# One weight sum of a seven-product output projection stored whole, and split into its two parts later

## The chip, the cores and the metric

The kernel runs on one core of a Trainium2 chip. The time is the device time of one execution in microseconds (us); the kernel before took 1030.03 us, the median of three runs (1028.07 to 1033.39). The engines are TensorE (PE; its weight loads are listed as PEld), VectorE (DVE), ScalarE (ACT), GpSimd (POOL) and SyncE (SP), which here issues most of the DMAs.

## What is computed

One block of a hybrid model on a sequence of 1024 tokens of width 1024, in float32. A state-space branch (SSD) and an attention branch of eight heads each give 1024 columns; the two stand side by side and go through an output projection, whose result is added to the input and normalized:

```python
mixed = jnp.concatenate([y_ssd, y_attn.astype(h.dtype)], axis=-1)   # 1024 x 2048
h = h + jnp.einsum('bse,ed->bsd', mixed, w_out[layer])              # w_out: 2048 x 1024
return rms_norm(h, final_norm_gain)
```

The change is in that projection alone.

## The kernel before

**Precision in two parts.** A float32 matrix product is made of three matmuls. Each operand is split into a high part, rounded to the engine's fp32r format by an ACT copy, and a low part, the operand less its high part, by a DVE subtraction. The sum high x high + high x low + low x high is gathered in PSUM. `product` (L854) does this for a tile of 128 tokens by 512 columns: eight steps k of three matmuls (L863, L864, L865), 24 in all; a product of four tiles has 96.

**Seven products.** The projection is taken as a 2 x 2 block product with seven block products in place of eight. The right operands are three quarters of w_out as they are (b11, b21, b22) and four sums T1 to T4 of quarters: T3 = b22 - b12, T2 = T3 + b11, T4 = b21 - T2, T1 = b22 - T2. The left operands are quarters of the transposed `mixed` and sums S1 to S4 of them. At the end stand, in this order, the products a12 x b21, S3 x T3 (its last two tiles), S2 x T2, S1 x T1, S4 x b22 and a22 x T4.

**Where the sums are made.** `sums_t(k)` (L695) makes T1 to T4 for rows 128k to 128k+127 of the quarters. It is a generator; the loop over the heads calls `next_sums` (L739) between the query tiles of attention, so the sums are made piece by piece from about 370 to 790 us. T1, T2 and T4 are split there by `split` (L702): an ACT copy to the high part (L704), its store to DRAM (L705), a DVE subtraction to the low part (L706), its store (L707). T3 is stored whole (L711). Behind T come the sums of the left operand S3 (`sums_s`, L723), in the same four buffers of tag K.

**How they come back.** `load_b` (L779) loads stored parts straight into two tiles of 128 x 8 x 512 of tag u (four of those exist, so a right operand can be loaded when the one two products back is done): eight DMAs of 512 KB. `prep_b` (L766) loads a whole operand in pieces of two k (512 KB) into raw tiles, and splits each piece by an ACT copy (L774) and a DVE subtraction (L775). There are two raw tiles, so the third piece is loaded when the first is split. T3 and the plain quarters go through `prep_b`, T1, T2 and T4 through `load_b`.

**Order.** The program is written in one order, and a planner that simulates time (L1052) then sets the order in which each engine takes its instructions; on the chip each engine keeps to it. All loads of the end go through `dma_next` (L753), in a chain on SP in the order in which they are written. The last attention head's output is needed in S2 as well, so a part of S2 is made late (L672, `s2`). `add` (L937) adds a finished product to the output rows `xr` and frees its PSUM buffer, of which there are two (`mm`); `end_p2` (L966) does it for a12 x b21, the loop at L980 for S2 x T2.

Of the kernel before, what the change touches and what calls it, by code (L numbers as in the profile page):

```python
# [8 lines left out]
F32 = mybir.dt.float32  # L9
# [6 lines left out]
P = 128  # L16
# [4 lines left out]
HALF = 512  # L21
# [17 lines left out]
def kernel(  # L39
# [12 lines left out]
    dma = nc.sync.dma_start  # L52
# [5 lines left out]
    dram = ctx.enter_context(tc.tile_pool(name="dram", bufs=1, space=bass.MemoryType.DRAM))  # L58
# [13 lines left out]
    def tH(shape, dt=F32, name="tH"):  # L72
        return big_tile("H", 5, shape, dt, name)

    def tK(shape, dt=F32, name="tK"):
        return big_tile("K", 4, shape, dt, name)
# [605 lines left out]

    NB = 8

    t_d = {n: dram.tile([NB, P, HALF] if n == 3 else [NB, 2, P, HALF], F32, name=f"t_d{n}") for n in (1, 2, 3, 4)}
    s3_d = dram.tile([NB, P, HALF], F32, name="s3_d")

    def w_quarter(kh, nh):
        src = w_out2[kh * D : (kh + 1) * D, nh * HALF : (nh + 1) * HALF]
        return src.rearrange("(a p) c -> a p c", p=P)  # L690

    def pin(ins):
        return tc.keep_in_program_order(ins)

    def sums_t(k):  # L695

        b11, b12, b21, b22 = (tK([P, HALF], name=f"b{i}{j}{k}") for i in range(1, 3) for j in range(1, 3))
        for raw, i, j in ((b22, 1, 1), (b12, 0, 1), (b11, 0, 0), (b21, 1, 0)):
            pin(dma(raw, w_quarter(i, j)[k]))
        yield  # L700

        def split(n, b):  # L702
            hi = tH([P, HALF], F32R, f"t{n}h{k}")
            A.activation(hi, b, AF.Copy)  # L704
            dma(t_d[n][k, 1], hi.bitcast(F32))  # L705
            V.tensor_tensor(b.bitcast(F32R), b, hi.bitcast(F32), ALU.subtract)  # L706
            dma(t_d[n][k, 0], b)  # L707

        t1, t2, t3, t4 = b22, b11, b12, b21
        pin(V.tensor_tensor(t3, t1, t3, ALU.subtract))  # L710
        dma(t_d[3][k], t3)  # L711
        V.tensor_tensor(t2, t3, t2, ALU.add)
        yield
        pin(V.tensor_tensor(t4, t4, t2, ALU.subtract))
        V.tensor_tensor(t1, t1, t2, ALU.subtract)
        yield
        split(2, t2)
        yield
        split(4, t4)
        split(1, t1)  # L720
        yield

    def sums_s():  # L723
# [11 lines left out]
        yield  # L735

    sums = [sums_t(k) for k in range(NB)] + [sums_s()]

    def next_sums():  # L739
# [13 lines left out]
    def dma_next(dst, src):  # L753

        if queued and queued[0] is not None:
            with tc.issue_after(queued[0]):
                queued[0] = dma(dst, src).ins
        else:
            ins = dma(dst, src).ins
            if queued:  # L760
                queued[0] = ins

    def b_tiles(name):
        return [big_tile("u", 4, [P, NB, HALF], F32R, f"{name}_{n}") for n in ("hi", "lo")]

    def prep_b(name, src, makers):  # L766

        hi, lo = b_tiles(name)
        k = 0
        for make, n in makers:  # L770
            raw = make([P, n, HALF], name=f"r{name}{k}")
            dma_next(raw, src[k : k + n].rearrange("a p c -> p a c"))
            cut = slice(k, k + n)
            A.activation(hi[:, cut, :], raw, AF.Copy)  # L774
            V.tensor_tensor(lo[:, cut, :], raw, hi[:, cut, :].bitcast(F32), ALU.subtract)  # L775
            k += n
        return hi, lo

    def load_b(name, parts):  # L779

        hi, lo = b_tiles(name)
        for k in range(0, NB, 2):
            for n, part in ((1, hi), (0, lo)):
                dma_next(part[:, k : k + 2, :].bitcast(F32), parts[k : k + 2, n].rearrange("a p c -> p a c"))
        return hi, lo
# [11 lines left out]
    def prep_a(name, q, cuts, piece):  # L797

        hi = big_tile("whi", 2, [P, NB, 256], F32R, f"{name}h{q}")
        lo = big_tile("wlo", 2, [P, NB, 256], F32R, f"{name}l{q}")  # L800
        for k0, k1 in zip(cuts, cuts[1:]):
            raw = piece(q, k0, k1 - k0)
            cut = slice(k0, k1)
            A.activation(hi[:, cut, :], raw, AF.Copy)
            V.tensor_tensor(lo[:, cut, :], raw, hi[:, cut, :].bitcast(F32), ALU.subtract)
        return hi, lo
# [3 lines left out]
    def piece_of(th, kh, make):  # L810
        def piece(q, k0, n):
            raw = make([P, n, 256], name=f"ra{th}{kh}{q}{k0}")
            load_a(raw, th, kh, q, k0, n)
            return raw

        return piece
# [105 lines left out]
    def load_x(t0):  # L922
        for t in range(t0, t0 + 4):
            dma_next(xts[t].rearrange("p n c -> p (n c)"), xf[t * P : (t + 1) * P, :])
# [48 lines left out]
    for i, _, _, ps in product(a7, b7, (2, 3)):  # L973
        A.activation(p7[i // 2][:, i % 2, :], ps, AF.Copy)
    a2.append(prep_a("a12", 1, BY2, piece_of(0, 1, tK)))
    b6 = load_b("t2", t_d[2])
    load_x(4)
    end_p2((2, 3))
    a6 = [prep_a("s2", q, BY4_LAST, piece_s2) for q in range(2)]
# [77 lines left out]
```

## Time and profile before

| what | us |
|---|---|
| median of three runs | 1030.03 |
| the profiled execution | 1029.03 |
| its span (first to last instruction) | 1027.3 |
| PE busy | 1000.8 |
| DVE busy | 657.7 |
| ACT busy | 530.1 |
| the S2 x T2 product on PE | 931.9 to 953.4 |

The span is what the profile's views divide up; the 1.7 us by which the execution is longer lie around it. Busy time of PE holds overlapping matmuls: one of 512 columns is listed with 0.39 us, but the next starts about 0.23 us later. A wait counts where PE is the one that waits.

### The profile page before, as it was taken

What the parts mean: (1) busy time and instruction counts of PE and PEld (TensorE: products, weight loads), DVE (VectorE), ACT (ScalarE), POOL (GpSimd) and SP (SyncE); (2) the same over time, 40 slices, a digit from 0 to 9 for tenths busy, and PEclk for the clock granted to TensorE, in tenths of its full rate; (3) what the DMA queues carried; (4) which work ended last, traced back from release to release, by engine and by line L of the source; (5) the groups of instructions that cost most, each with busy time, mean ns of one, the idle gap of its engine ahead of it and who ended that gap; (6) DMA issues with size and microseconds to landing.
All of it is one profiled execution on the core that took longest, in us unless ns stands there. A gap on an engine that the chain in (4) does not pass through costs nothing.

```text
span 1027.3 us, 16300 instructions
## 1 busy us (share of the span) xinstructions
PE 1000.8 (97%) x6214; PEld 887.4 (86%) x6214; DVE 657.7 (64%) x1373; ACT 530.1 (52%) x1161; POOL 93.0 (9%) x133
## 2 busy tenths in 40 slices
PE   7999999999999999999999999999999999999997
PEld 6988888879997999889998889988899888778786
DVE  5475678756566368385573873847817867756974
ACT  6535466844466446455554564546625656542331
POOL 5100024200232100000000000000000000000001
PEclk9999999999999999999999999999999999999999
DMA  7111224221224424242144322336304863579693
GB/s 298 41 41 64 70 65 134 82 62 62 84 84 121 123 73 140 89 141 63 72 165 123 83 93 81 135 118 182 93 22 147 257 213 115 167 243 390 237 313 118
DMA packets 72311, 133.65 MB, mean 130 GB/s; under 512 B 6107, under 2 KB 30504, under 8 KB 72232
## 3 DMA queue, kind: packets, MB, share of 16 engines
q1 hardware_dynamic: 69928, 128.41, 38.0%
q10 hardware_dynamic: 2304, 4.20, 1.1%
q8 instruction: 49, 0.80, 0.3%
q14 instruction: 30, 0.25, 0.1%
HBM read 94.76 MB, written 29.43 MB: 121 GB/s over the span
## 4 chain that ended last, share of the span: by engine, by line
PE 88%; DMA 4%; DVE 3%; ACT 2%; issue 2%; POOL 0%; SPq 0%; POOLq 0%; DVEq 0%; ACTq 0%
PE mm L210 9%; PE mm L211 9%; PE mm L212 9%; PE mm L219 8%; PE mm L221 8%; PE mm L220 8%; PE o L619 5%; PE S L567 5%; PE mm L863 5%; PE mm L864 5%; PE mm L865 5%; PE S L451 3%; PE tp L612 3%; PE S L460 1%; PE S L464 1%
## 5 line engine op out<-in xcount | busy, mean ns | idle before, releaser
L573 DVE CUSTOM_DVE_ANT_0 s<-S,dist 128x256 f32<-128x256 f32 (+7 forms) x128 | 95.0, 753 | 97.0 <-PE S L567 92.7
L591 ACT ACTIVATE s<-s,small 128x256 f32<-128x256 f32 (+7 forms) x128 | 98.5, 771 | 58.4 <-DVE small L583 58.1
L210 PE MATMUL mm<-uh,hi_qk 128*128 128x512 f32 x256 | 101.3, 396 | 0.0
L212 PE MATMUL mm<-uh,lo_qk 128*128 128x512 f32 x256 | 101.1, 395 | 0.0
L211 PE MATMUL mm<-ul,hi_qk 128*128 128x512 f32 x256 | 100.6, 393 | 0.0
L567 PE MATMUL S<-k,q 128*128 128x512 f32 (+2 forms) x384 | 91.9, 356 | 0.9 <-DVE small L573 0.7
L615 ACT ACTIVATE wT<-tp 128x512 f32<-128x512 f32 (+2 forms) x96 | 46.6, 486 | 87.8 <-PE tp L612 87.5
L619 PE MATMUL o<-v,wT 128*128 128x128 f32 x576 | 79.9, 275 | 1.5 <-ACT wT L615 1.5
L619 PEld LDWEIGHTS o<-v,wT 128*128 128x128 f32 x576 | 74.3, 191 | 5.3 <-ACT wT L615 2.8
L219 PE MATMUL mm<-hi_v,uh 128*128 128x256 f32 x256 | 73.5, 287 | 0.4 <-DVE q L518 0.4
L221 PE MATMUL mm<-hi_v,ul 128*128 128x256 f32 x256 | 73.2, 286 | 0.0
L221 PE MATMUL mm<-hi_za,ul 128*128 128x256 f32 x256 | 73.2, 286 | 0.0
L220 PE MATMUL mm<-lo_v,uh 128*128 128x256 f32 x256 | 73.0, 285 | 0.0
L219 PE MATMUL mm<-hi_za,uh 128*128 128x256 f32 x256 | 72.9, 285 | 0.0
L220 PE MATMUL mm<-lo_za,uh 128*128 128x256 f32 x256 | 72.9, 285 | 0.0
L567 PEld LDWEIGHTS S<-k,q 128*128 128x128 f32 x384 | 63.7, 189 | 9.7 <-DVE small L573 2.0
L212 PEld LDWEIGHTS mm<-uh,lo_qk 128*128 128x128 f32 x256 | 48.1, 188 | 9.8 <-issue 0.2
L210 PEld LDWEIGHTS mm<-uh,hi_qk 128*128 128x128 f32 x256 | 48.1, 188 | 9.1 <-issue 0.2
L211 PEld LDWEIGHTS mm<-ul,hi_qk 128*128 128x128 f32 x256 | 48.2, 188 | 8.8
L219 PE MATMUL mm<-hi_z,uh 128*128 128x256 f32 x192 | 55.2, 287 | 0.0
L221 PE MATMUL mm<-hi_z,ul 128*128 128x256 f32 x192 | 55.0, 287 | 0.0
L220 PE MATMUL mm<-lo_z,uh 128*128 128x256 f32 x192 | 54.9, 286 | 0.0
(290 smaller groups left out, 2654.6 us busy)
## 6 DMA issues: line engine op xcount, KB each, us to landing
m<-acs_d SPq DMA_DIRECT2D x16, 512.0 KB, 4.0
raw_qk<-in_w_blocks_dram SPq DMA_DIRECT2D x16, 512.0 KB, 4.4
q<-q SPq DMA_DIRECT2D x32, 256.0 KB, 3.5
b<-in_w_out_dram SPq DMA_DIRECT2D x32, 256.0 KB, 4.0
t_d<-b SPq DMA_DIRECT2D x32, 256.0 KB, 2.4
t_hi<-t_d SPq DMA_DIRECT2D x12, 512.0 KB, 9.0
t_lo<-t_d SPq DMA_DIRECT2D x12, 512.0 KB, 9.7
rb<-in_w_out_dram SPq DMA_DIRECT2D x10, 512.0 KB, 4.9
```

What stands on the lines that cost most here:

```text
L210: T.matmul(ps, hi[:, d, cut], uh[half][:, d, :], start=(d == 0), stop=False)
L211: T.matmul(ps, hi[:, d, cut], ul[half][:, d, :], start=False, stop=False)
L212: T.matmul(ps, lo[:, d, cut], uh[half][:, d, :], start=False, stop=(d == ND - 1))
L219: T.matmul(ps, uh[half][:, d, cut], hi[:, d, :], start=(d == 0), stop=False)
L220: T.matmul(ps, uh[half][:, d, cut], lo[:, d, :], start=False, stop=False)
L221: T.matmul(ps, ul[half][:, d, cut], hi[:, d, :], start=False, stop=(d == ND - 1))
L567: T.matmul(os[m], qs[half][m][:, part, qcut], ks[kh][:, m, :width], start=(part == 0), stop=(part == 1))
L573: V.tensor_tensor_reduce(out=s[:, :n], in0=ps[:, :n], in1=dist[:, S - n : S], op0=ALU.add, op1=ALU.max, scale=1.0, scalar=-3.0e38, accum_o ...
L591: A.activation(s[:, :n], s[:, :n], AF.Exp, bias=nb[:, m : m + 1], scale=slope, accum_out=sums[:, m, ii : ii + 1],)
L619: T.matmul(po[:, qcut], wT[:, kb, :], vs[kb // 4][:, kb % 4, vcut], start=(kb == 0), stop=(kb == i))
L863: T.matmul(ps[:, c0:c1], th[:, k, cut], bh[:, k, c0:c1], start=(k == 0), stop=False)
L864: T.matmul(ps[:, c0:c1], th[:, k, cut], bl[:, k, c0:c1], start=False, stop=False)
```

## The change

T2 is treated as T3 already is: `sums_t` stores the sum alone, eight pieces of 256 KB in place of sixteen, and the last product that needs it splits it with `prep_b` in four pieces, in raw tiles. The DRAM tensor loses its dimension of two. T1 and T4 are split and stored as before.

```diff
--- before.py
+++ after.py
@@ -682,7 +682,7 @@
 
     NB = 8
 
-    t_d = {n: dram.tile([NB, P, HALF] if n == 3 else [NB, 2, P, HALF], F32, name=f"t_d{n}") for n in (1, 2, 3, 4)}
+    t_d = {n: dram.tile([NB, P, HALF] if n in (2, 3) else [NB, 2, P, HALF], F32, name=f"t_d{n}") for n in (1, 2, 3, 4)}
     s3_d = dram.tile([NB, P, HALF], F32, name="s3_d")
 
     def w_quarter(kh, nh):
@@ -714,7 +714,7 @@
         pin(V.tensor_tensor(t4, t4, t2, ALU.subtract))
         V.tensor_tensor(t1, t1, t2, ALU.subtract)
         yield
-        split(2, t2)
+        dma(t_d[2][k], t2)
         yield
         split(4, t4)
         split(1, t1)
@@ -973,7 +973,7 @@
     for i, _, _, ps in product(a7, b7, (2, 3)):
         A.activation(p7[i // 2][:, i % 2, :], ps, AF.Copy)
     a2.append(prep_a("a12", 1, BY2, piece_of(0, 1, tK)))
-    b6 = load_b("t2", t_d[2])
+    b6 = prep_b("t2", t_d[2], [(raw_tile, 2)] * 4)
     load_x(4)
     end_p2((2, 3))
     a6 = [prep_a("s2", q, BY4_LAST, piece_s2) for q in range(2)]
```

On all engines the order is the same up to the first removed copy, and the planner has laid it out anew from there. Three places follow; numbers in names are buffer numbers, and differ for the same tile.

**DVE and PE at the S2 x T2 product.** DVE before, from the last low part of the left operand a12 on (`s` and `s2l` are S2, `p` and `xr` partial and final outputs, L672 the late part of S2):

```order
L805 TENSOR_TENSOR a12l_9284<-ra_9297,a12h_9283 128x512
L672 SCALAR_TENSOR_TENSOR s_9141<-tp,g_129,s_last 128x256
L672 SCALAR_TENSOR_TENSOR s_9151<-tp,g_129,s_last 128x256
L805 TENSOR_TENSOR s2l_9375<-s_9141,s2h_9374 128x256
L937 TENSOR_TENSOR xr_9124<-xr_9124,mm 128x512
L937 TENSOR_TENSOR xr_9124<-xr_9124,p_8544 128x512
L937 TENSOR_TENSOR xr_9125<-xr_9125,mm 128x512
L937 TENSOR_TENSOR xr_9125<-xr_9125,p_8544 128x512
L805 TENSOR_TENSOR s2l_9383<-s_9146,s2h_9382 128x1024
L945 TENSOR_SCALAR ssf<-ssf 128x1
```

DVE now:

```order
L805 TENSOR_TENSOR a12l_9252<-ra_9265,a12h_9251 128x512
L775 TENSOR_TENSOR t_lo<-rt_9272,t_hi 128x1024
L775 TENSOR_TENSOR t_lo<-rt_9276,t_hi 128x1024
L672 SCALAR_TENSOR_TENSOR s_9109<-tp,g_129,s_last 128x256
L672 SCALAR_TENSOR_TENSOR s_9119<-tp,g_129,s_last 128x256
L805 TENSOR_TENSOR s2l_9351<-s_9109,s2h_9350 128x256
L937 TENSOR_TENSOR xr_9092<-xr_9092,mm 128x512
L775 TENSOR_TENSOR t_lo<-rt_9280,t_hi 128x1024
L937 TENSOR_TENSOR xr_9092<-xr_9092,p_8512 128x512
L937 TENSOR_TENSOR xr_9093<-xr_9093,mm 128x512
L775 TENSOR_TENSOR t_lo<-rt_9284,t_hi 128x1024
L805 TENSOR_TENSOR s2l_9359<-s_9114,s2h_9358 128x1024
```

The four subtractions of T2's pieces (`t_lo<-rt`) stand in between: two ahead of the late part of S2, and one ahead of each of two later additions.

PE before, from matmul 16 of the product on (counted from 0; the two `mm` numbers are tiles 0 and 1):

```order
L864 MATMUL mm_9390<-t2_lo_9303,s2h0_9374 128x512
L865 MATMUL mm_9390<-t2_hi_9302,s2l0_9375 128x512
L863 MATMUL mm_9390<-t2_hi_9302,s2h0_9374 128x512
L863 MATMUL mm_9420<-t2_hi_9302,s2h0_9374 128x512
L864 MATMUL mm_9420<-t2_lo_9303,s2h0_9374 128x512
L865 MATMUL mm_9420<-t2_hi_9302,s2l0_9375 128x512
L863 MATMUL mm_9420<-t2_hi_9302,s2h0_9374 128x512
L864 MATMUL mm_9420<-t2_lo_9303,s2h0_9374 128x512
L865 MATMUL mm_9420<-t2_hi_9302,s2l0_9375 128x512
L863 MATMUL mm_9420<-t2_hi_9302,s2h0_9374 128x512
L864 MATMUL mm_9420<-t2_lo_9303,s2h0_9374 128x512
L864 MATMUL mm_9390<-t2_lo_9303,s2h0_9374 128x512
```

PE now:

```order
L864 MATMUL mm_9366<-t2_lo_9271,s2h0_9350 128x512
L865 MATMUL mm_9366<-t2_hi_9270,s2l0_9351 128x512
L863 MATMUL mm_9366<-t2_hi_9270,s2h0_9350 128x512
L863 MATMUL mm_9396<-t2_hi_9270,s2h0_9350 128x512
L864 MATMUL mm_9396<-t2_lo_9271,s2h0_9350 128x512
L865 MATMUL mm_9396<-t2_hi_9270,s2l0_9351 128x512
L863 MATMUL mm_9396<-t2_hi_9270,s2h0_9350 128x512
L864 MATMUL mm_9396<-t2_lo_9271,s2h0_9350 128x512
L865 MATMUL mm_9396<-t2_hi_9270,s2l0_9351 128x512
L863 MATMUL mm_9396<-t2_hi_9270,s2h0_9350 128x512
L864 MATMUL mm_9396<-t2_lo_9271,s2h0_9350 128x512
L865 MATMUL mm_9396<-t2_hi_9270,s2l0_9351 128x512
```

Before, tile 1 is started behind the first matmul of step 6 and broken off after eight matmuls; now all of the first four steps of tile 1 stand ahead of the rest of tile 0. In the S1 x T1 product before, tile 1 is likewise taken up when tile 0 has six of its eight steps, and the two end in turns; now tile 0 is finished first, then tile 1.

**ACT at the gate of head 4.** Before (`hi_za` is the conversion of gate weights, `s` an exponential of attention scores, `tTa` the copy of a gated head's output out of PSUM, `wT` a copy of transposed attention weights):

```order
L591 ACTIVATE s_7247,sums_7191<-s_7247,small_7232 128x768
L201 ACTIVATE hi_za_8119<-raw_za_8121 128x8x128
L201 ACTIVATE hi_za_8119<-raw_za_8123 128x8x128
L591 ACTIVATE s_7282,sums_7191<-s_7282,small_7271 128x896
L659 ACTIVATE tTa_7168<-tp,g_129 128x512
L517 ACTIVATE q_7486<-mm 64x512
```

Now:

```order
L591 ACTIVATE s_7215,sums_7163<-s_7215,small_7204 128x768
L201 ACTIVATE hi_za_8087<-raw_za_8089 128x8x128
L201 ACTIVATE hi_za_8087<-raw_za_8091 128x8x128
L591 ACTIVATE s_7219,sums_7163<-s_7219,small_7204 128x768
L659 ACTIVATE tTa_7140<-tp,g_129 128x512
L591 ACTIVATE s_7254,sums_7163<-s_7254,small_7243 128x896
```

The 896-column exponential stood ahead of `tTa` and now stands behind it.

**ACT at the first product's left operand.** Before (`a11h` are its conversions, one for each load; `za`, `k` are of the projections):

```order
L615 ACTIVATE wT_8022<-tp 128x512
L591 ACTIVATE s_8752,sums_8740<-s_8752,small_8741 128x128
L804 ACTIVATE a11h_8489<-ra_8491 128x512
L615 ACTIVATE wT_8022<-tp 128x384
L804 ACTIVATE a11h_8489<-ra_8495 128x512
L321 ACTIVATE za_8368<-mm 128x512
L804 ACTIVATE a11h_8489<-ra_8499 128x512
L804 ACTIVATE a11h_8489<-ra_8503 128x512
L615 ACTIVATE wT_8075<-tp 128x512 x2
```

Now:

```order
L615 ACTIVATE wT_7990<-tp 128x512
L804 ACTIVATE a11h_8457<-ra_8459 128x512
L528 ACTIVATE k_8331<-mm 64x512
L804 ACTIVATE a11h_8457<-ra_8463 128x512
L591 ACTIVATE s_8720,sums_8708<-s_8720,small_8709 128x128
L804 ACTIVATE a11h_8457<-ra_8467 128x512
L528 ACTIVATE k_8331<-mm 64x512
L615 ACTIVATE wT_7990<-tp 128x384
L804 ACTIVATE a11h_8457<-ra_8471 128x512
L591 ACTIVATE s_8739,sums_8708<-s_8739,small_8732 128x256
L615 ACTIVATE wT_8043<-tp 128x512
```

Ahead of the copy `wT` of 384 columns stood one conversion and now stand three; the fourth stands ahead of the next `wT` in both.

## Rows read from the trace of the kernel before

**Rows 1.** The page's engine summary: busy us, share of the span, count of instructions.

```profile
PE 1000.8 (97%) x6214; PEld 887.4 (86%) x6214; DVE 657.7 (64%) x1373; ACT 530.1 (52%) x1161; POOL 93.0 (9%) x133
```

**Rows 2.** Busy us (count): PE, PEld, DVE, ACT, POOL; clock; DMA share; GB/s.

```profile
365.00:905.00 540.00, 530.68 (x3477) 481.04 (x3476) 351.05 (x931) 289.27 (x658) 18.39 (x30) 1.00 0.39 125
920.00:940.00 20.00, 20.00 (x92) 16.56 (x91) 11.44 (x22) 7.24 (x13) 1.34 (x1) 1.00 0.93 356
940.00:960.00 20.00, 20.00 (x90) 16.53 (x90) 19.26 (x27) 3.18 (x3) 0.00 (x0) 1.00 1.06 376
```

**Rows 3.** Who waited for whom, PE, 365 to 905: total us, times, longest.

```profile
PE tp L612 <- ACT wT L615: 2.4, 3, 1.5
PE tp L612 <- ACT tTa L659: 1.7, 1, 1.7
PE o L619 <- ACT wT L615: 1.5, 2, 1.0
PE mm L863 <- ACT a12h L664: 1.1, 1, 1.1
```

**Rows 4.** Instructions of tile t2h: duration ns least/median/most, first and last start us.

```profile
L704 ACT ACTIVATE t2h<-b x8: 613/620/633, 373.5 to 765.0; 128x512 fp32r<-128x512 f32 x8
L706 DVE TENSOR_TENSOR b<-b,t2h x8: 672/684/693, 379.1 to 775.6; 128x512 fp32r<-128x512 f32 x8
```

**Rows 5.** Same view, tile t_hi: the two conversions of T3, made by prep_b.

```profile
L774 ACT ACTIVATE t_hi<-rt x4: 1047/1062/1063, 838.3 to 846.6; 128x1024 fp32r<-128x1024 f32 x4
L775 DVE TENSOR_TENSOR t_lo<-rt,t_hi x4: 1201/1214/1215, 839.5 to 848.6; 128x1024 fp32r<-128x1024 f32 x4
```

**Rows 6.** DMA issues (KB each, median us to landing); then all on t_d.

```profile
t_hi<-t_d SPq DMA_DIRECT2D x12, 512.0 KB, 9.0
rt<-t_d SPq DMA_DIRECT2D x4, 512.0 KB, 5.3
...
DMA to landing us min/median/max: 2.0/3.2/11.3
```

**Rows 7.** Instructions of tile t_hi: PE's matmuls of the T2 product.

```profile
L863 PE MATMUL mm<-t_hi,s2h x32: 389/389/389, 931.9 to 953.0; 128*128 128x512 f32 x32
```

**Rows 8.** Timeline of ACT behind 920: start us, us, instruction.

```profile
922.68 0.62 ACT L804 ACTIVATE a12h<-ra 128x512 fp32r<-128x512 f32 x1
```

**Rows 9.** Timeline of DVE, 916 to 979; in brackets the idle time before.

```profile
916.78 0.96 DVE L838 TENSOR_TENSOR s<-s,s3b 128x768 f32<-128x768 f32 x1 [0.88 <-DMA s3b<-s_d]
...
925.98 0.88 DVE L672 SCALAR_TENSOR_TENSOR s<-tp,g,s_last 128x256 f32<-128x256 f32 x2 [0.66 <-ACT tTa L659]
...
930.37 0.42 DVE L805 TENSOR_TENSOR s2l<-s,s2h 128x256 fp32r<-128x256 f32 x1 [3.51 <-ACT s2h L804]
...
939.34 0.69 DVE L982 TENSOR_TENSOR p<-p,mm 128x512 f32<-128x512 f32 x1 [3.38 <-PE mm L865]
...
963.14 0.69 DVE L937 TENSOR_TENSOR xr<-xr,mm 128x512 f32<-128x512 f32 x1 [1.96 <-PE mm L865]
...
964.88 0.68 DVE L937 TENSOR_TENSOR xr<-xr,mm 128x512 f32<-128x512 f32 x1
...
976.08 2.35 DVE L805 TENSOR_TENSOR s4l<-ra,s4h 128x1024 fp32r<-128x1024 f32 x2
```

**Rows 10.** Groups of instructions behind 885: PE's first of the T1 product, idle last.

```profile
L863 PE MATMUL mm<-t_hi,s1h 128*128 128x512 f32 x32 | 12.5, 391 | 1.0 <-DVE xr L937 1.0
```

**Rows 11.** Timeline of ACT, 733 to 735.

```profile
733.53 1.03 ACT L591 ACTIVATE s<-s,small 128x896 f32<-128x896 f32 x1
...
734.55 0.67 ACT L659 ACTIVATE tTa<-tp,g 128x512 f32<-128x512 f32 x1
```

**Rows 12.** Timeline of ACT, 829 to 836.

```profile
829.62 0.47 ACT L615 ACTIVATE wT<-tp 128x384 f32<-128x384 f32 x1
...
832.53 0.63 ACT L804 ACTIVATE a11h<-ra 128x512 fp32r<-128x512 f32 x1
834.98 0.63 ACT L804 ACTIVATE a11h<-ra 128x512 fp32r<-128x512 f32 x1 [1.82 <-DMA ra<-tt_d]
```

## The prediction

> **What bounds the kernel now.** I read the page's engine summary first: TensorE (PE) has work in flight for 97% of the span [rows 1], so whatever this change does must show up as a PE wait that goes or one that comes. None of its matmuls is removed or added. The second view is the busy time of the stretches [rows 2]: in both stretches after 920 us, where the changed load sits, PE has no idle time at all, while VectorE (DVE) is busy 11.4 of 20 us in the first and 19.3 of 20 in the second, and the DMA engines are as good as full in both (a share of 1.06 is overlap of packets, not spare room). So DVE has about 8 us free right where the change puts new DVE work, and nearly none behind it. The granted clock is 1.00 in all three. The third view, who waited for whom on PE from 365 to 905 us (the stretch in which the weight sums are made), says what could be gained there: four groups of waits on ScalarE (ACT), 2.4 + 1.7 + 1.5 + 1.1 = 6.7 us [rows 3]. No PE wait in it names a T2 instruction.
>
> **The change, part by part.** First, what goes from the attention stage: eight ACT copies of 0.62 us (5.0 us) and eight DVE subtractions of 0.68 us (5.5 us) [rows 4], and of the 16 stores of T2, 256 KB each, eight. Neither engine is the bound there (ACT busy 289 and DVE 351 of 540 us [rows 2]), and PE waits for none of these; cost now 0, gain 0. Bounds: nothing above 0 from the removal itself; below, no more than the 6.7 us of rows 3.
>
> Second, the order. The planner lays the whole order out anew from the first removed copy on, so the removal also moves what does not depend on it. Two places matter.
>
> At 731 to 735 us PE stands 1.7 us for the copy tTa [rows 3]: ACT does two conversions and an exponential before it, the last starting at 733.53, so tTa starts at 734.55 [rows 11]. In the new order tTa stands ahead of that exponential. It can start 1.02 us earlier; I take -1.0 us. Bounds: -1.7 (the whole wait) and 0 (PE then waits for the next copy instead).
>
> At 829 to 836 us ACT, which takes its instructions in order, stands for loads of the first product's left operand. Before, one conversion (a11h) stands ahead of the copy wT of 384 columns, which runs at 829.62; in the new order three do. The third ran at 832.53 + 0.63 = 833.16, so that copy is late by up to 833.16 - 829.62 = 3.5 us [rows 12]. But the copy after it, wT of 512, stands behind the fourth conversion in both orders (834.98 [rows 12]), and the new order adds only one small exponential before it. PE has to wait for that later copy anyway, so what counts is nearer to the small end: I take +0.7 us, an estimate: the exponential is 256 columns wide, and one of 896 takes 1.02 us with its readout [rows 11], so it lies between 0.3 (by width) and 1.0. Bounds 0 and +3.5.
>
> Third, the end. Removed: eight loads of 512 KB into t_hi and t_lo, each pair waiting for the buffers that the last s3 product frees. Added: four loads of 512 KB into two raw tiles, four ACT conversions of 1.06 us and four DVE subtractions of 1.21 us (prices of the same helper on T3 [rows 5]): 4.2 us ACT, 4.9 us DVE. The question is whether piece k is there when PE asks. PE starts the T2 product at 931.9 and its last t_hi,s2h matmul, number 93 counted from 0, starts at 953.0: 0.227 us each [rows 7]. In PE's new order piece 2's t_lo is matmul 13 (934.9), piece 3's t_hi matmul 18 (936.0), then tile 1 begins with matmul 19 (936.2), and piece 3's t_lo comes only at 31 (938.9).
>
> Supply: loads 0 and 1 wait for raw tiles alone, the second of them for the subtraction that ended at 916.78 + 0.96 = 917.7 [rows 9]; at 5.3 us each, as below, both are there by 923.0. ACT finishes the copy before the first conversion at 922.68 + 0.62 = 923.3 [rows 8], so t_hi of pieces 0 and 1 end at 924.4 and 925.4. DVE, idle for 0.66 us by 925.98, is free at 925.3 [rows 9]; t_lo of 0 and 1 end at 926.5 and 927.7, and only that frees the two raw tiles for loads 2 and 3. A load of this kind took 5.3 us in the attention stage, 9.0 us in the train of eight that it replaces here, and the longest of any on this tensor 11.3 [rows 6]. The train is gone, so I take the row that it is nearest to, 5.3: piece 2 lands at 931.8, ACT to 932.9, DVE to 934.1, 0.8 us before its matmul. Piece 3 lands at 933.0, ACT to 934.1; DVE does two additions of 0.69 first (935.5, and the second frees the accumulator tile 1 wants at 936.2), then t_lo to 936.7, 2.2 us early. Cost 0. Bounds: nothing, and +5.3 for a landing of 11.3 (rival B).
>
> The Trainium skill, page "DMA: Bandwidth & Descriptors", section "Anatomy of one DMA", gives about 2.0 us plus the bytes at 436 GB/s for a DMA of the GpSimd path, an estimate of 3.2 us here. By it piece 2 would be 2.1 us earlier still and the sum would not change, only rival B would become less likely; the trace has 5.3 and 9.0 us for this size, well above it.
>
> Now DVE behind it. The two accumulator rows s2l (927.7 + 0.88 for the two operations on the last head's tile, + 0.42) and the first addition end at 929.7, earlier than the 930.37 + 0.42 of today, which waited 3.51 for ACT [rows 9]. From 936.7 on follow s2l of 1.21, 0.95 (by its width, an estimate) and 0.42, an addition of 0.69 and two operations on single columns (0.3, an estimate): 940.2. Today DVE has idled 3.38 us by 939.34 [rows 9]; so the 4.9 us are paid from idle time, and the step after starts 0.9 us late. That is taken back, because today's PE order interleaves tiles 0 and 1 of the T1 product: DVE waits 1.96 us for tile 0 at 963.14, does a 1.22 us subtraction in between, and frees the accumulator only at 964.88 + 0.68, for which PE waits 1.0 us [rows 9, 10]. In the new order the two tiles run one after the other and both additions stand together. DVE work from 939.34 to 961.18 (963.14 less the wait) is 21.8 us, so it comes to 962.0 in the new order; both additions end at 963.4, and PE wants that accumulator at 931.9 + 144 x 0.227 = 964.6. The 1.0 us goes. Next late is s4l: 976.08 - 963.14 = 12.9 us of unbroken work [rows 9] put it at 974.9 to 976.1, and PE wants it at 931.9 + 194 x 0.227 = 975.9: 0.2 us, within the rounding. So -1.0 us; bounds -1.4 and 0.
>
> **The sum.** The profiled execution took 1029.03 us (span 1027.3, and 1.7 around it): 1029.03 - 1.0 + 0.7 - 1.0 = 1027.7. The median of the runs, 1030.03, stands 1.0 above that execution and would come to 1028.7. I say **1028.2 us**, the middle. A measurement of this kernel can tell about 0.5% from no change, 5.15 us, so this is no change: under 1024.9 is faster, over 1035.2 slower.
>
> **Rival A, the new order clears the attention waits.** If all 6.7 us of rows 3 go, not only the 1.0 counted: 1028.2 - 5.7 = 1022.5 us. For it: ACT and DVE have 10.5 us less to do there, and every one of these waits is for ACT. Against it: they are seven waits, most of them far from any T2 copy, and a new order opens waits as well as closing them.
>
> **Rival B, the ring of two raw tiles is late (slower).** Place: matmul 13 of the T2 product, with loads 2 and 3 issued only at 926.5 and 927.7. It decides from a landing of 6.1 us on (5.3 plus the 0.8 to spare). At 11.3 us piece 2 is ready at 926.5 + 11.3 + 1.06 + 1.21 = 940.1, 5.2 us late, DVE is behind by the same and gives PE another 0.7 or so at s4l: 1028.2 + 5.9 = 1034.1 us. For it: 9.0 is the median where these loads run in a train, and the x rows follow at once. Against it: nothing else is queued when they are issued.
>
> **Rival C, three conversions ahead of one copy.** Place: 829 us, price the full 3.5 us instead of 0.7: 1031.0 us. It decides if PE needs the 384-wide copy before the fourth load lands. The change brings no time in the attention stage and loses what the end gains.
>
> **How the numbers follow.** Forecast 0.50 (its own range 1026 to 1031), A 0.22, C 0.16, B 0.12. Faster is A, 0.22. Slower is the upper part of B (landings above 12 us, or B and C together at 1037) and orders as bad as that elsewhere: 0.12. The rest, 0.66, is no change. The range must leave out no more than 0.2: half of A lies below 1022 and about 0.08 of B and worse above 1034, so **1022.0 to 1034.0**.
>
> **What the profile of the changed kernel would show.** Right: four rt loads on t_d after 914 us that land in 4 to 6 us; PE with no wait before t_hi or t_lo matmuls between 920 and 960; no wait of about 1 us at the third tile of the T1 product; tTa ahead of its exponential and a shorter PE wait there; DVE over 14 of 20 us in 920 to 940. Wrong: a PE wait for t_lo of T2 (B), a PE wait of 3 us or more near 833 us (C), or the sum of PE waits on ACT from 365 to 905 under 2 us (A).

## The result and the profile after

The changed kernel takes **1034.05 us** (median of 14 runs, 1032.23 to 1037.23), the kernel before 1028.01 us in 14 runs beside them: a ratio of **1.0056 (1.0047 to 1.0065)**, 5.8 us slower. The forecast was 1028.2 us, with a range of 1022.0 to 1034.0 and "no change"; the time lies just above the range. The forecast stood on a median of 1030.03 us for the kernel before and on terms of -1.0, +0.7 and -1.0, which make -1.3 us; the measured change is +5.8. The time is near the 1034.1 us of rival B by chance: nothing of rival B happened.

The profiled execution took 1034.07 us, its span 1032.2 against 1027.3 us. PE is as busy as before [rows 1]:

```profile
PE 1001.7 (97%) x6214; PEld 888.9 (86%) x6214; DVE 660.1 (64%) x1369; ACT 529.8 (51%) x1157; POOL 90.9 (9%) x133
```

The whole loss is there before PE uses the changed load. PE's matmuls of the S2 x T2 product (tile t_hi; least, median and most ns, first and last start in us):

```profile
L863 PE MATMUL mm<-t_hi,s2h x32: 389/389/390, 938.3 to 959.4; 128*128 128x512 f32 x32
```

Before, the first started at 931.9 [rows 7]: PE comes to this product 6.4 us late. From there to the end of the span it took 1027.3 - 931.9 = 95.4 us before and takes 1032.2 - 938.3 = 93.9 now. The end gains 1.5 us, and the stages ahead of it lose 6.4.

Who waited for whom on PE, from 365 us to this point (us in total, times, longest):

```profile
PE tp L612 <- ACT wT L615: 5.9, 5, 2.7
PE mm L863 <- ACT a12h L804: 2.0, 1, 2.0
PE tp L612 <- ACT tTa L659: 1.9, 2, 1.5
PE o L619 <- ACT wT L615: 1.3, 2, 1.1
PE mm L863 <- ACT a12h L664: 1.1, 1, 1.1
PE mm L219 <- DVE q L518: 0.5, 1, 0.5
PE S L567 <- DVE small L573: 0.4, 1, 0.4
```

These are 13.1 us. The same view of before, taken to its 931.9 us, comes to 9.1, most of it in the groups of [rows 3]. What is new is 2.7 us for a copy `wT` and 2.0 us for `a12h`, with `tTa` now waited for in two places. So 4.0 of the 6.4 us are waits. In this execution the granted clock can account for the rest (stretches of the changed kernel; us, busy us and counts of PE, PEld, DVE, ACT, POOL, clock, DMA share, GB/s):

```profile
736.00:738.00 2.00, 0.46 (x4) 0.22 (x3) 1.90 (x5) 1.95 (x5) 0.00 (x0) 0.95 0.79 289
738.00:740.00 2.00, 1.93 (x10) 1.94 (x10) 1.97 (x4) 1.56 (x10) 0.00 (x0) 0.50 1.00 362
740.00:742.00 2.00, 2.00 (x14) 2.00 (x13) 1.38 (x8) 1.05 (x3) 0.31 (x2) 0.70 0.45 118
818.00:820.00 2.00, 2.00 (x14) 1.87 (x15) 1.88 (x7) 1.76 (x4) 0.00 (x0) 1.00 0.89 280
890.00:892.00 2.00, 1.18 (x3) 0.75 (x4) 1.38 (x3) 2.00 (x7) 0.00 (x0) 0.85 0.42 163
892.00:894.00 2.00, 2.00 (x6) 1.52 (x6) 1.03 (x3) 1.97 (x9) 0.00 (x0) 0.50 0.01 4
894.00:896.00 2.00, 2.00 (x9) 1.59 (x8) 0.66 (x4) 0.10 (x2) 0.87 (x2) 0.80 0.00 0
```

Twice the clock falls to the lower level (0.50 is 1.2 GHz), right behind new waits: PE stood 0.40 us until 735.8 and 1.61 us until 738.1, and 1.96 us until 890.8. In the execution of before it is 1.00 from 365 to 905 and from 920 to 960 us [rows 2]. Summed as (1 - clock) x 2 us these windows lose up to 3.4 us, part of it while PE stood anyway; 2.4 us are what the waits leave to be explained. Whether the clock costs as much in the other runs is taken up with e8.

The places, from the timeline of the changed kernel (start us, us, instruction, in brackets the idle time before and what ended it):

```profile
601.93 0.66 PE L612 MATMUL tp<-ident,s 128*128 128x128 f32 x4 [1.49 <-ACT tTa L659]
...
735.08 0.67 ACT L659 ACTIVATE tTa<-tp,g 128x512 f32<-128x512 f32 x1
735.65 1.03 ACT L591 ACTIVATE s<-s,small 128x896 f32<-128x896 f32 x1
735.80 0.66 PE L612 MATMUL tp<-ident,s 128*128 128x128 f32 x4 [0.40 <-ACT tTa L659]
...
737.42 0.60 ACT L615 ACTIVATE wT<-tp 128x512 f32<-128x512 f32 x1
...
738.07 0.48 PE L612 MATMUL tp<-ident,s 128*128 128x128 f32 x1 [1.61 <-ACT wT L615]
...
815.60 1.06 ACT L774 ACTIVATE b_hi<-rb 128x1024 fp32r<-128x1024 f32 x1 [0.37 <-DMA rb<-in_w_out_dram]
...
817.29 0.60 ACT L615 ACTIVATE wT<-tp 128x512 f32<-128x512 f32 x1
...
817.94 0.44 PE L612 MATMUL tp<-ident,s 128*128 128x128 f32 x2 [2.71 <-ACT wT L615]
...
889.02 1.13 ACT L591 ACTIVATE s<-s,small 128x1024 f32<-128x1024 f32 x1
...
890.16 1.66 ACT L804 ACTIVATE a12h<-ra 128x512 fp32r<-128x512 f32 x3
...
890.82 0.50 PE L863 MATMUL mm<-b_hi,a12h 128*128 128x512 f32 x1 [1.96 <-ACT a12h L804]
```

- At 600 us PE waits 1.49 us for the copy `tTa` of an earlier head.
- At the gate of head 4 `tTa` does stand ahead of the exponential of 896 columns and PE waits 0.40 us for it in place of 1.66. But that exponential now stands ahead of the next `wT`, and PE waits 1.61 us for that.
- At 815 us the conversion `b_hi` of the first product's right operand waits for its load and stands ahead of `wT`: PE waits 2.71 us.
- At 889 us an exponential of 1024 columns stands ahead of three conversions `a12h`: PE waits 1.96 us.

At the end the mechanism was that of the steps. The view of the raw tiles `rt` (all eight, the four of T3 and the four of T2):

```profile
L757 SPq DMA_DIRECT2D rt<-t_d x4: 359/366/371, 922.0 to 934.3; - x4
...
DMA to landing us min/median/max: 3.5/5.4/6.9
```

and the third and fourth piece of T2, the later load of S1, and the reader of PE's third tile:

```profile
936.85 1.06 ACT L774 ACTIVATE t_hi<-rt 128x1024 fp32r<-128x1024 f32 x1 [1.76 <-DMA rt<-t_d]
...
937.95 1.22 DVE L775 TENSOR_TENSOR t_lo<-rt,t_hi 128x1024 fp32r<-128x1024 f32 x1 [0.57 <-ACT t_hi L774]
...
939.43 1.06 ACT L774 ACTIVATE t_hi<-rt 128x1024 fp32r<-128x1024 f32 x1 [1.52 <-DMA rt<-t_d]
...
940.52 1.22 DVE L775 TENSOR_TENSOR t_lo<-rt,t_hi 128x1024 fp32r<-128x1024 f32 x1 [0.16 <-ACT t_hi L774]
...
948.47 1.23 DVE L846 TENSOR_TENSOR ra<-ra,s 128x1024 f32<-128x1024 f32 x1 [1.12 <-DMA ra<-tt_d]
```

The landing times are those of all eight; read one by one, T2's four loads took 6.6, 5.6, 3.7 and 5.1 us. Loads 2 and 3 were issued at 933.1 and 934.3, so 5.2 and 4.0 us ahead of the product (5.4 and 4.2 by the steps). `t_lo` of piece 2 ends at 939.2; PE wants it at matmul 13, 938.3 + 13 x 0.227 = 941.3. It is 2.1 us early, and 1.6 us of that is its landing in 3.7 us in place of 5.3. PE has no wait at all behind 938.3 us; the 1.0 us for `xr` [rows 10] is gone.

### The profile page after: what moved, and what is told of

The parts are those of the page before. It is cut to its first block, busy times and chain, and to the rows that moved or that the text cites. A ratio compares the mean times of both kernels' runs of the same rounds, so it can differ in the third digit from the quotient of the medians.

```text
span 1032.2 us, 16271 instructions
## 1 busy us (share of the span) xinstructions
PE 1001.7 (97%) x6214; PEld 888.9 (86%) x6214; DVE 660.1 (64%) x1369; ACT 529.8 (51%) x1157; POOL 90.9 (9%) x133
## 4 chain that ended last, share of the span: by engine, by line
PE 89%; DMA 4%; DVE 3%; ACT 2%; issue 1%; POOL 0%; POOLq 0%; SPq 0%; DVEq 0%; ACTq 0%
PE mm L210 9%; PE mm L211 9%; PE mm L212 9%; PE mm L219 8%; PE mm L220 8%; PE mm L221 8%; PE o L619 5%; PE S L567 5%; PE mm L863 5%; PE mm L865 5%; PE mm L864 5%; PE tp L612 3%; PE S L451 3%; DMA s_d<-a 1%; PE S L460 1%
## 5 line engine op out<-in xcount | busy, mean ns | idle before, releaser
L612 PE MATMUL tp<-ident,s 128*128 128x128 f32 x288 | 47.7, 274 | 7.8 <-ACT wT L615 5.9
```

What stands on the lines that cost most here:

```text
L612: T.transpose(pt[:, b * P : (b + 1) * P], sb[0][:, (b0 + b) * P : (b0 + b + 1) * P], ident)
```

## The experiments

**Theory N**: the loss is the attention stage's new order on ACT, DVE and PE, nothing else. **Rival L**: the late load and split at the end cost it. **Rival D**: less work in the stage, or T2's buffers coming free at other moments, makes it slower whatever the order. Every ratio is to runs of the kernel before taken beside that run on the same chip (their median was 1027.7 to 1028.4 us), so ratios are to be compared, not medians. The clock is the mean over all runs of a kernel. The last three columns come from one profiled execution, whose time can lie some us off the median (e4's took 1026.4): all PE waits from 365 us to PE's first matmul of S2 x T2, the start of that matmul ("T2 starts"), and the span behind it ("end").

| run | ratio to before (95%) | median us | clock | PE waits | T2 starts | end |
|---|---|---|---|---|---|---|
| before | 1 | 1027.7 to 1028.4 | 0.998 | 9.1 | 931.9 | 95.4 |
| changed | 1.0056 (1.0047 to 1.0065) | 1034.05 | 0.996 | 13.1 | 938.3 | 93.9 |
| e1 changed end alone | 0.9979 (0.9967 to 0.9991) | 1026.73 | 0.998 | 8.3 | 930.4 | 94.2 |
| e2 changed attention alone | 1.0072 (1.0054 to 1.0090) | 1035.96 | 0.995 | 14.2 | 937.5 | 96.4 |
| e3 work kept | 0.9998 (0.9984 to 1.0012) | 1028.88 | 0.998 | 8.3 | 932.3 | 94.6 |
| e4 changed, no yield | 1.0007 (0.9993 to 1.0020) | 1029.37 | 0.996 | 8.4 | 930.2 | 94.4 |
| e5 before, no yield | 1.0121 (1.0104 to 1.0138) | 1041.48 | 0.994 | 16.8 | 944.3 | 95.4 |
| e6 before, yield moved | 1.0022 (1.0011 to 1.0033) | 1030.34 | 0.998 | 13.0 | 935.0 | 95.5 |
| e7 changed, a12h first | 1.0058 (1.0045 to 1.0072) | 1033.95 | 0.996 | 11.5 | 933.1 | 94.8 |
| e8 changed, both places | 1.0035 (1.0022 to 1.0047) | 1032.03 | 0.998 | 12.4 | 935.9 | 94.4 |
| e9 changed, old order | 1.0010 (0.9997 to 1.0023) | 1028.84 | 0.997 | 9.1 | 932.4 | 96.5 |
| e10 changed, splits swapped | 1.0056 (1.0036 to 1.0077) | 1033.32 | 0.996 | 13.5 | 938.7 | 94.6 |
| e11 changed, yield moved | 1.0007 (0.9997 to 1.0018) | 1028.80 | 0.997 | 8.9 | 931.9 | 95.0 |
| e12 end, low part | 0.9994 (0.9984 to 1.0005) | 1027.45 | 0.998 | 8.7 | 931.0 | 94.4 |

### The two halves apart

e1, the changed end behind the old attention stage:

```diff
-    b6 = load_b("t2", t_d[2])
+    b6 = prep_b("t2", t_d[2][:, 1], [(raw_tile, 2)] * 4)
```

> Leaves out: the low part of T2 in the last product but three (the end reads the stored high part alone and splits that, so its low part is zero). The attention stage is that of the kernel before, instruction for instruction on every engine; only the end is the changed one. Theory N (the loss is the attention stage's new order, worth +6.4 us by 920 us; the end itself gains 1.5 us): ratio to before 0.9985, about 1026.5 us, PE waits of 365 to 905 us as before (8.9 us in all), no 1.0 us wait for xr in the T1 product, granted clock 1.00 at 730 to 900 us. Rival L (the late load and split at the end cost the 6 us): ratio 1.005 or more, 1033 us or more, with PE waits behind 905 us.

e2, the changed attention stage in front of the old loads:

```diff
-        split(2, t2)
+        dma(t_d[2][k], t2)
...
-    b6 = load_b("t2", t_d[2])
+    b6 = load_b("t2", t_d[2], whole=True)
```

> Leaves out: the split of T2 (the end loads the sum as it is into both parts, with the eight loads of the kernel before). The attention stage is that of the changed kernel, instruction for instruction; the end's loads are those of before. Theory N: slower than the changed kernel by what its end gained: ratio to before 1.007 (1.0055 to 1.008), about 1035.3 us, the same PE waits at 600, 736, 815 and 889 us as the changed kernel, the 1.0 us wait for xr back. Rival L: ratio 1.000, about 1028 us.

Both came out as theory N had them: 0.9979 and 1.0072. The loss goes with the attention stage alone, and rival L falls. In e2 the wait for `xr` is back (1.2 us). PE's first T2 matmul shows it, in e1 and in e2 (the number before the comma is its start):

```profile
L863 PE MATMUL mm<-t_hi,s2h x32: 389/389/389, 930.4 to 951.5; 128*128 128x512 f32 x32
```

```profile
L864 PE MATMUL mm<-t_hi,s2h x32: 389/389/501, 937.5 to 958.8; 128*128 128x512 f32 x32
```

### Work or order

e3 keeps the eight copies and subtractions, whose results nobody reads:

```diff
+        hi = tH([P, HALF], F32R, f"t2h{k}")
+        A.activation(hi, t2, AF.Copy)
         dma(t_d[2][k], t2)
+        V.tensor_tensor(hi, t2, hi.bitcast(F32), ALU.subtract)
+        dma(scrap[k], hi.bitcast(F32))
```

> Stores T2 whole and splits it at the end as the change does, but keeps the eight ACT copies, the eight DVE subtractions and a second store of 256 KB each in the attention stage, whose results nobody reads; the order of the attention stage is then that of the kernel before. Theory N: ratio 0.9985, about 1026.5 us, faster than the changed kernel by 7 us although it does 10.5 us more work on ACT and DVE. Rival D (the stage gets slower because something wants the removed work's time or buffers, whatever the order): cannot be slower than before in this kernel either, so both give the same here; Rival L: 1033 us or more.

It measured 0.9998, 0.0013 above what was expected. The expectation was wrong in one thing: the order is not that of before. The planner made a third one, near to it (1110 of the 1161 ACT instructions of before stand in the same sequence). So e3 does not tell work from order by itself; e9 does.

e4, e5 and e6 are new orders without a new amount of work: one `yield` of the generator taken out or moved.

```diff
         dma(t_d[2][k], t2)
-        yield
         split(4, t4)
```

> The changed kernel without the yield behind the store of T2, so the split of T4 and T1 comes one query tile earlier and the planner lays the attention stage out anew once more; the end is the changed kernel's. Theory N (which copies PE waits for is a matter of each order): the PE waits of 365 to 905 us stand at other places than the changed kernel's (600, 736, 815, 889 us) and the time can fall anywhere from 1024 to 1036 us. Rival D (less work in the stage costs 6 us whatever the order): 1034 us within 1, ratio 1.005 to 1.007.

```diff
         split(2, t2)
-        yield
         split(4, t4)
```

> The kernel before, T2 split and stored in both parts as it was and the end as it was, without the yield between the split of T2 and that of T4: not one instruction more or less, only another moment of writing, so that the planner lays the attention stage out anew. Theory N: the time leaves that of before by more than 0.2% in either direction (1022 to 1036 us), and its PE waits of 365 to 905 us stand at other places. Rival D (time follows work): ratio 1.000 within 0.0015.

```diff
         split(2, t2)
-        yield
         split(4, t4)
+        yield
         split(1, t1)
-        yield
```

> The kernel before, with the yield moved from ahead of the split of T4 to behind it: the same instructions again, a third order. Theory N: again anywhere from 1022 to 1036 us, and not the time of the run without the yield. Rival D: ratio 1.000 within 0.0015 in both.

e5 is the plainest result of all: the kernel before, with not one instruction changed, is **1.2% slower** when a `yield` is taken out, which changes only the order. Its PE waits from 365 us to its T2 product:

```profile
PE tp L612 <- ACT wT L615: 4.6, 6, 1.9
PE mm L862 <- ACT a12h L803: 3.9, 1, 3.9
PE o L619 <- ACT wT L615: 3.0, 3, 1.2
PE mm L210 <- DVE k L529: 1.7, 2, 1.4
PE tp L612 <- ACT tTa L659: 1.4, 1, 1.4
```

These five groups of seven are 14.6 us, and all seven 16.8, where all of before are 9.1; a single wait of 3.9 us is for the same `a12h` as in the changed kernel. The waits are thus 7.7 of the 12.4 us by which its T2 product starts later. e4 shows the reverse: the changed kernel's own instructions, laid out once more, give back 5 of the 5.8 us. e6 lies between, 0.2% slower. Rival D in its first form, by which time follows work, falls: the same instructions gave 1, 1.0022 and 1.0121.

e10 and e11 give the changed kernel two more orders:

```diff
-        split(4, t4)
-        split(1, t1)
+        split(1, t1)
+        split(4, t4)
```

> The changed kernel with the splits of T4 and T1 written in the other order: ACT and DVE change eight pairs of rows each, PE's order stays the same to the last matmul. Theory N (it is PE's and its suppliers' order that counts): ratio to before 1.0056 within 0.0015, as the changed kernel. If a re-written program scatters by several us whatever its order on PE, the ratio lies elsewhere.

```diff
         dma(t_d[2][k], t2)
-        yield
         split(4, t4)
+        yield
         split(1, t1)
```

> The changed kernel with the yield between the splits of T4 and T1 instead of ahead of both: the same instructions, a third order of the attention stage for them. Theory N: anywhere from 1022 to 1042 us (the two orders of before and this one's sisters span 1028 to 1041), with PE waits at places of its own, and the end as in the changed kernel (no wait for xr). Rival D: ratio 1.0056 within 0.0015.

e10, whose PE order is the changed kernel's to the last matmul, has its time, 1.0056. e11, with another order, has 1.0007. So this rewriting, which left PE's order alone, did nothing; other orders of PE and of what feeds it did.

### The old order with the changed instructions

e9 holds the four engines' issue order by edges that carry no semaphore; `ORDER` lists, for each engine, places in the program as "first+count":

```diff
+    for engine, runs in ORDER.items():
+        mine, last = traced[engine], None
+        for r in runs.split():
...
+                    tc.add_manual_dep(
+                        mine[n],
+                        mine[last].name,
...
```

> The changed kernel whole (T2 stored as the sum, split at the end, no work left over), but ACT, DVE, PE and SP held to the order of the run with the changed end alone by issue-order edges: in the attention stage that is the order of the kernel before less the removed rows, at the end the changed kernel's. Theory N (the loss is the order alone, not the removed work): ratio to before 0.998 (0.9965 to 0.9995), about 1026 us, 7 us faster than the changed kernel with the same instructions; PE waits of 365 to 905 us those of before. Rival D (less work in the stage makes it slower, or T2's buffers come free at a worse time): ratio 1.004 or more.

1.0010 (0.9997 to 1.0023): with the very instructions of the changed kernel 4.7 us come back, and the interval lies wholly below the changed kernel's. **This shows that the order is the cause of most of the loss**, and rival D, which had 1.004 or more here, falls in its second form too. The edges hold SP's DMA issues as well, so e9 does not tell the order of the DMA issues from that of the other three engines. Its waits in the attention stage are those of before, eight groups of together 9.1 us; the first four:

```profile
PE tp L752 <- ACT wT L755: 2.2, 4, 1.1
PE tp L752 <- ACT tTa L799: 1.7, 1, 1.7
PE o L759 <- ACT wT L755: 1.4, 2, 1.0
PE mm L1003 <- ACT a12h L804: 1.1, 1, 1.1
```

But it is not the 0.998 that was expected. Its profile says why, for that execution: the clock fell behind the 1.7 us wait for `tTa`, where it had not in the profile of before, and S1's load came late enough for DVE to idle 3.09 us, so that PE waited for `xr` again.

The clock window (columns as above), the row of DVE's timeline, and the group of PE's waits behind 932.4 us:

```profile
730.00:750.00 20.00, 18.23 (x130) 16.86 (x129) 16.05 (x37) 13.68 (x31) 1.20 (x2) 0.91 0.30 93
```

```profile
944.53 1.23 DVE L986 TENSOR_TENSOR ra<-ra,s 128x1024 f32<-128x1024 f32 x1 [3.09 <-DMA ra<-tt_d]
```

```profile
PE mm L1003 <- DVE xr L1077: 0.9, 2, 0.7
```

In the changed kernel that load cost DVE 1.12 us of idle time. The end is without slack there, and whether it gains is up to that landing.

e12 asks whether e1 was flattered because T2's second part was all zeros in it:

```diff
-    b6 = prep_b("t2", t_d[2][:, 1], [(raw_tile, 2)] * 4)
+    b6 = prep_b("t2", t_d[2][:, 0], [(raw_tile, 2)] * 4)
```

> As the run with the changed end alone, with the same order on every engine, but the end splits the stored low part in place of the stored high part. Leaves out: the high part of T2. In that run the second part of T2 was all zeros; here it is not, and nothing else differs. Theory Z (the 2 us by which that run beat the changed kernel in the old order come from operands that are zero): ratio to before 1.000 to 1.001, about 1028.5 us. Theory W (they come from elsewhere: the removed rows, landings): ratio 0.998 again, about 1026 us.

0.9994 (0.9984 to 1.0005) lies between the two theories and overlaps both e1 and e9. It stays open how much of e1's 2.2 us the end really gives; by the three runs in the old order (0.9979, 0.9994, 1.0010) the end is worth between 2 us gained and 1 us lost. In the new order the changed kernel is 1.6 us faster than e2, with overlapping intervals. The Trainium skill, page "TensorE: Matmul & The Clock Gate", section "Seeing it yourself", warns against zeroed operands in such trials, but for a limiter that it says one busy core never trips; by that page the zeros of e1 should not count, and e12 neither confirms nor excludes it.

### Two of the places mended

e7 moves one ACT row, e8 also keeps `b_hi` behind the `wT` at 815 us:

```diff
+                with tc.issue_after(found_a["a12", 0]) if (h, n) == (HEADS - 1, S) else ExitStack():
                     A.activation(
                         s[:, :n],
...
+            with tc.issue_after(found_w[HEADS - 2, 5, 0]) if (name, k) == ("b11", 4) else ExitStack():
                 A.activation(hi[:, cut, :], raw, AF.Copy)
```

> The changed kernel with one ACT row moved: the exponential of 1024 columns (head 7, tile 7, first map) is held behind the three conversions a12h that PE waits for at 889 us; all else of the order stays. Theory N: the wait for a12h shrinks from 2.0 to 0.6 us, and the stretch of half clock behind it (1.7 us) goes: 1.4 to 3.1 us faster than the changed kernel, ratio to before 1.0026 to 1.0043. Rival E (PE then waits elsewhere for the exponential that is now late): ratio 1.005 to 1.006, as the changed kernel.

> As the run before it, and the third conversion of b11, which waits for its load ahead of the copy wT of 512 that PE waits for at 815 us, is held behind that copy. The planner lays out anew from 812 us on. Theory N: the wait at 815 us shrinks from 2.7 to 1.6 us or less; with the 1.4 to 3.1 us of the place at 889 us ratio 1.001 to 1.0035. Rival E: ratio 1.005 or more.

In e7's profile the wait went from 2.0 to 0.5 us, as expected:

```profile
PE tp L613 <- ACT wT L616: 5.9, 5, 2.7
PE mm L865 <- ACT a12h L805: 0.5, 1, 0.5
```

and the clock held at 1.00; that execution took 1029.98 us. But its four other runs took 1033.3 to 1034.8 us, and the ratio is the changed kernel's, 1.0058, where 1.0026 to 1.0043 was expected. That is rival E's number, but no new wait shows in the profile (11.5 us in all against 13.1). The mean clock of its runs is 0.996 as in the changed kernel, but the run of 1033.3 had 0.998; the four have no trace. So e7 shows that the wait could be taken away and not that the time follows. e8 came in at 1.0035, the edge of what was expected: the wait at 815 us shrank to 1.3 us, but 1.2 us for `k` appeared just ahead of it:

```profile
816.50 0.50 PE L569 MATMUL S<-k,q 128*128 128x256 f32 x2 [1.20 <-DVE k L529]
...
818.29 0.44 PE L615 MATMUL tp<-ident,s 128*128 128x128 f32 x2 [1.29 <-ACT wT L618]
```

**How much of the loss is the clock stays open.** For a part of some 2 us: the mean clock of the changed kernel is 0.0022 below that of before and of e8, and 0.0022 x 1032 us = 2.3 us, near the 2.4 that the waits leave in its profile; and e6, with 13.0 us of waits in its profile and the mean clock of before, is only 2.3 us slower than before. Against it: four of the changed kernel's 14 runs had a clock of 0.998, as the runs of before have in the mean, and took 1033.73 to 1034.03 us, no less than its three runs at 0.995 (1033.14 to 1034.07); and e4 and e11, whose mean clocks are 0.996 and 0.997, took 1029.37 and 1028.80 with waits of 8.4 and 8.9 us.

No run that keeps the whole computation is faster than the kernel before by more than its interval; e1 is, and leaves a part out.

## Why the prediction was wrong

- **What bounds the kernel** held: PE is 97% busy in both, and in the profiled executions the difference is PE waits and clock.
- **What goes from the attention stage ("cost now 0, gain 0")** held for the work itself. e9, without that work in the old order, has PE's waits of before.
- **"Second, the order." and "Two places matter."** This is the step that failed. The order changes from about 370 to 920 us, and I priced two places in it, both of them places where PE waited before, at -1.0 and +0.7, together -0.3 us. The new waits came at other places, of 1.5 us at 600, 2.7 at 815 and 2.0 at 889 us, and the sum of PE's waits rose by 4.0 us. e9 puts 4.7 us of the loss down to the order.
- **The tTa term** (-1.0) was right about its row and wrong about the sum: the wait for `tTa` shrank by 1.3 us, and the next copy, behind the exponential that had been passed, was late by as much. The bound of 0, "PE then waits for the next copy instead", was the case.
- **The a11h term** (+0.7) did not come: the three conversions stood ahead of the 384-column copy as read, but PE waited 0.24 us for it and nothing for the next, for which it had waited 1.52 before. Rival C fell with it. PE's rows, now and before:

```profile
832.39 0.94 PE L619 MATMUL o<-v,wT 128*128 128x128 f32 x6 [0.24 <-ACT wT L615]
```

```profile
836.15 0.66 PE L612 MATMUL tp<-ident,s 128*128 128x128 f32 x4 [1.52 <-ACT wT L615]
```

- **Rival A** had the sign wrong. It took the waits of before as a sum that a new order could only give back; "a new order opens waits as well as closing them" stood in its own text and got no price. "Orders as bad as that elsewhere" shared a chance of 0.12 with the upper part of rival B, and nothing was added to the sum for them.
- **The clock** was read as 1.00 in all three stretches and left out. In the profiled execution two stretches at the lower level came with the new waits; what they cost over all runs is open, as said above.
- **The end** (-1.0) was right in its mechanism: loads landing in 3.7 to 6.6 us (5.3 forecast), `t_lo` of piece 2 2.1 us before its matmul (0.8 forecast), the `xr` wait gone; the profile shows -1.5. But the gain rests on S1's load, which the steps had not timed: where it came late, in e9, the `xr` wait was back.

## What to carry to other kernels

Where a planner lays the order out from simulated times, a small edit can re-draw everything behind it, and here, with PE 97% busy, the draw was worth more than the edit: the same instructions spread over 1.2% (the kernel before) and 0.5% (the changed one). Size this scatter by re-drawing the kernel before without changing its work, and widen the range by it to both sides; then judge an edit under a held order (e9 against before), not under whichever order it happened to get. If the order found is good, hold it.

## What the runs showed of the hardware

The granted clock differs from one execution to the next of the same program: over the 23 runs of before beside e9 it is 0.994 to 1.000, and the run at 0.994 took 1032.8 us, the one at 1.000 took 1026.8. In e9 it fell at 730 to 750 us behind a wait of 1.7 us for `tTa`; behind the same wait it stayed at 1.00 in the profile of before, and behind 2.7 us at 815 us of the changed kernel it did too. So a wait's length alone did not decide it here, and no run here tells what did. The Trainium skill, page "TensorE: Matmul & The Clock Gate", section "Part 1: The HAM clock gate (the "warmup" mystery)", says that the gate keeps its own time, whatever moment the kernel starts at, and that one kernel therefore differs from run to run; the spread of these 23 runs agrees, though nothing here shows that this is its cause.
